# One encoder layer on one core: seven-product units in every down pair of two FFN parts, one cast and one store moved, two more dummy matmuls

## The chip, the cores and the metric

The kernel runs on one core of a Trainium2 chip. The metric is device time in microseconds (us). The kernel before took 1159.08 us in the median of three runs (1156.46 to 1161.56). One execution was profiled, and everything that is read from the trace below is of that one.

Engines are named as the profile names them: PE multiplies matrices (PEld is its load of weights, which overlaps the multiplication), DVE does element-wise vector work, ACT does casts, copies and activation functions, POOL is used here mainly to issue DMAs, and SP issues most of the DMAs.

## The reference, cut to what matters

One encoder layer over 256 tokens of width 2048, in float32. It has a mixing sub-layer (neighbourhood attention beside a recurrent block), then a dense SwiGLU feed-forward layer of inner width 5632, then a gated embedding. Only the feed-forward layer (FFN) is touched by the change, beside the first microseconds of the kernel:

```python
fn = rms_norm(h, g_ffn_pre[i])
ff = (jax.nn.silu(fn @ w_ffn_gate[i]) * (fn @ w_ffn_up[i])) @ w_ffn_down[i]
h = h + rms_norm(ff, g_ffn_post[i])
```

`w_ffn_gate` and `w_ffn_up` are 2048 x 5632, `w_ffn_down` is 5632 x 2048.

## The kernel before, in words

**Precision.** PE works here on a reduced 32-bit type. So each float32 operand is split into a rounded part and a remainder (`hi` and `lo` of the activations, `wh` and `wl` of the weights), and each block product takes three matmuls: hi x wh, lo x wh and hi x wl. One block product multiplies 128 tokens by 128 contraction rows by 512 columns. ACT makes `wh` with a cast (L630, `hi_stream`), DVE makes `wl` with a subtraction (L643, `lo_stream`), and both do it for each weight tile as it arrives. A weight tile is 128 partitions x 2 contraction blocks x 512 columns, 512 KB in float32.

**Groups.** The FFN is worked off in three parts of 4, 4 and 3 feature chunks of 512 (`PARTS`). In each part, every feature chunk f is one *group*: its gate chunk and its up chunk, accumulated together over 16 contraction blocks. Then follow two *down groups*, which multiply the part's features with `w_ffn_down`: the first makes output chunks 0 and 1 (c = 0), the second makes chunks 2 and 3 (c = 2). A group takes its contraction blocks two at a time. In a plain *pair*, two token tiles, two contraction blocks and two column chunks make eight block products (24 matmuls, `products`, L677 to L679). A *seven-product unit* makes the same result from seven block products (21 matmuls, `product`, L688 to L690) with sums and differences of blocks, in three pieces:

- `four_products`: four products, whose results are combined once per group by `made_of_four` (four DVE and two ACT operations on accumulators);
- `two_products`: two products;
- `one_product`: one product of each unit; the units 0 and 1 of a group share one weight tile here, unit 2 has its own.

The pieces of *four* are put among the last pairs of the group before (table `FOURS`: after how many pairs), the *two* and *one* pieces among the first pairs of their own group (table `TAKEN`). For its sums a unit needs three more DVE additions of 512 columns (L578, L582, L588, `sum_stream`), one DMA on POOL's queue that adds 256 KB of a weight block from memory to a block in the core (L599, `last_sum`), and seven blocks of weights to cast and subtract instead of four. It also needs sums of the activations: for the features of a part, `mid_sums` makes them with four DVE subtractions and a split (L1761, L306, L308).

Gate and up groups have three units from f = 2 on. Of the down groups, those of c = 0 have two units (contraction pairs 0 and 2 of the part) and those of c = 2 three (0, 2 and 4). In the last part c = 0 has two and c = 2 none.

**Features.** When a gate and up group ends, `up_post` makes the feature chunk on DVE, transposes it in 32 x 32 blocks (L334), and moves the blocks into place with sixteen small DMAs into the tile `mT` (L344, on POOL's queue). When the last has landed, `carried` casts `mT` into `mid0h` and `mid0l` (ACT L306, DVE L308; the digit is the part), and `mid_sums` follows. `mT` has one buffer: the next feature's DMAs wait until the sums of this one are made.

**Order.** Every engine works its queue in order. The order is written by a planner (`Plan`) while the program is built: each stream of work is a generator that yields its next operation with a modelled cost; `plan.add(..., ready)` says from when a task may be placed. For a DMA, `_run` sets the task's `ready` to the modelled start of that DMA, and `plan.now` is a scratch time that `done(event)` copies into an event and that is set anew when the task goes on. So the modelled times decide which cast stands ahead of which in ACT's queue; at run time an operation waits for its real data, and all that stand behind it on that engine wait too. There are five buffers for split weight tiles (`wh` and `wl` by fours, and `w`), so casts can run at most some tiles ahead of PE.

**Spill.** After the mixing sub-layer the residual `h` (two tiles of 1 MB) is stored to memory by `spill_h` (L1608), because its two buffers are used again: the first for loaded weight tiles called `lower` (the second tile of a four piece), the other for the sums of features (`sums`).

**Start.** `WARM` dummy matmuls on a constant tile run before the first weights are there (L2101). Each is executed in two passes.

Of the kernel before, what the change touches and what calls it, by code (L numbers as in the profile page):

```python
# [18 lines left out]
NT = S // P  # L19
# [18 lines left out]
PARTS = ((0, 4), (4, 8), (8, 11))  # L38
SEVEN_KS = (0, 2, 4)
RING = 5  # L40
DOWN_KS = {0: (0, 2), 2: (0, 2, 4)}
SEVEN_F = range(2, 11)

SWAPPED = [
    (lambda f: (("w_ffn_gate", f), ("w_ffn_up", f)), SEVEN_F, SEVEN_KS),
    *(
        (lambda c: (("w_ffn_down", c), ("w_ffn_down", c + 1)), (c,), [4 * f0 + k for k in ks])
        for f0, _ in PARTS for c, ks in DOWN_KS.items() if not c or f0 != PARTS[-1][0]
    ),
]  # L50

# [18 lines left out]
SOON = 2.0  # L70
ADDED = 6.0
AHEAD = 5
ISSUE = 160
WARM = 9


class Event:


    t = None  # L80
# [141 lines left out]
def dve(n, take=None, give=None):  # L222
    return ("dve", COST["dve"] + 0.00104 * n, None, take, give)
# [6 lines left out]
def dma(kb, take=None):  # L230
    return ("dma", kb / 340.0, None, take, None)
# [3 lines left out]
def layer(ctx: ExitStack, tc: tile.TileContext, a: dict, out: bass.AP):  # L235
# [3 lines left out]
    at = ctx.enter_context(tc.tile_pool(name="at", bufs=1))  # L239
    ps = ctx.enter_context(tc.tile_pool(name="ps", bufs=4, space=bass.MemoryType.PSUM))  # L240
    plan = Plan(wr=R_BUFS, w=W_BUFS, sm=SM_BUFS, acc=4, ev=1, mid=2, bt=2, m2=1, mt=1, sq=1, T0=1, T1=1, T4=1, **{f"{s}{j}": n for s, m, n in (("p", 5, 1), ("t", 3, 0)) for j in range(m)}, wr0=1, w0=1)
# [61 lines left out]
    def split(hi, lo, src, n, give=None):  # L303

        yield act(n)
        nc.scalar.copy(hi, src)  # L306
        yield dve(n, give=give)
        nc.vector.tensor_tensor(out=lo, in0=src, in1=f32(hi), op=ALU.subtract)  # L308
# [42 lines left out]
    def by_tile(v):  # L351
        return v.rearrange("p k (t q) -> p k t q", t=NT)
# [13 lines left out]
    def done(event):  # L366
        event.t = plan.now
# [47 lines left out]
    def seg(chunk, w, n0, lhs, ks, first=True, last=True, after=None):  # L415
        s = (chunk, lhs, ks, first, last, after, len(tiles))
        for k, _ in ks:
            tiles.append((w, k, n0))
        segs.append(s)
# [11 lines left out]
    class Group:  # L431
# [47 lines left out]
        def issue(self, nxt):  # L479
            if self.own is None:  # L480
                self.own = []
            self.twos = []
            if nxt:
                nxt.own = []
            n, m = len(self.rest), len(self.rest) - self.apart
            more = []
            for js in (range(0, 2), range(2, len(self.sevens))):
                more += [lambda j=j: self.two(j) for j in js if self.sevens]
            for js in (range(0, 2), range(2, len(self.sevens))):
                more += [lambda js=js: self.one(js)] if js and self.sevens else []  # L490
            taken = list(TAKEN.get((len(self.sevens), n), ()))

            def take():
                for _ in range(taken.pop(0) if taken else 0):
                    more.pop(0)()

            take()
            for i, k in enumerate(self.rest[:m]):
                for j, at in enumerate(FOURS[n, len(nxt.sevens)] if nxt and nxt.sevens else ()):
                    if i == at:  # L500
                        nxt.four(j)
                if i >= self.ahead:
                    self.pair(i)
                if nxt and nxt.apart and i == 1:
                    nxt.pair(0)
                    nxt.ahead = 1
                take()
            for ch, w, n0 in self.chunks if self.apart else ():
                seg(ch, w, n0, self.lhs, self.rest[m:], first=False)

    TAKEN = {(3, 5): (0, 2, 3), (2, 6): (0, 1, 1, 1), (2, 4): (0, 2, 1)}
    FOURS = {(8, 3): (3, 5, 7), (5, 3): (2, 3, 4), (6, 3): (3, 4, 5), (5, 2): (2, 4), (6, 2): (3, 5)}
    fours = {}

    raws, his, los = {}, {}, {}
# [290 lines left out]
    ev_unmerged = Event()  # L806
# [709 lines left out]
    def next_norm(sub, nxt, rstd, ev_rstd, g_next):  # L1516
# [51 lines left out]
        if sub is mix:  # L1568
            plan.add(spill_h(), plan.now)
# [28 lines left out]
        ).tile([NT, P, D], F32, name=f"part{i}")  # L1598
        for i in range(2)
    ]  # L1600
    ev_spilled, ev_back = Event(), Event()

    def spill_h():
        for e in hF.ev:
            yield e
        for t in range(NT):
            yield dma(1024)
            nc.sync.dma_start(spill[t], t2["h"].tiles[t])  # L1608
        done(ev_spilled)

    half_spill = ctx.enter_context(
        tc.tile_pool(name="half_spill", bufs=1, space=bass.MemoryType.DRAM)
# [51 lines left out]
    hF = Act()  # L1664
# [54 lines left out]
    def up_post(f, mid, kk0, g, soon):  # L1719

        def post(ch):
            yield g.free
            e = es.pop(f)
            for t in range(NT):
                yield dve(N)
                nc.vector.scalar_tensor_tensor(
                    out=e[:, t, :], in0=ch.accs[t], scalar=rstd_f[:, t : t + 1], in1=e[:, t, :],
                    op0=ALU.mult, op1=ALU.mult,
                )
            ch.release()  # L1730
            there = Event()
            mT = yield from moved(e, there, "mt", mT_tile, pool=(0, 2) if soon else range(4))
            plan.free["mid"].append(plan.now)
            yield there
            plan.add(carried(mid, kk0, mT), plan.now + (0.5 if soon else 3.0), -SOON if soon else 0.0)
        return post

    def carried(mid, kk0, mT):
        summed = any(kk0 <= kx < kk0 + 4 for kx in mid.ev_sums)
        for b in range(0, 4, 2):  # L1740
            kk = kk0 + b
            i, j = divmod(kk, 8)
            hi, lo = mid.tiles(i)
            yield from split(
                *(by_tile(x[:, j : j + 2, :]) for x in (hi, lo)), mT[:, b : b + 2], 2 * S,
                give="mt" if b and not summed else None,
            )
            mid.pair(kk)
        if summed:
            plan.add(mid_sums(mid, kk0, mT), plan.now + (20.0 if mid.name[-1] == str(2) else 0.0))  # L1750

    def mid_sums(mid, kk0, mT):

        yield ev_unmerged if kk0 else ev_spilled
        kxs = [kx for kx in DOWN_KS[2] if kk0 <= kx < kk0 + 4]
        m = 2 * len(kxs)
        a11, a12 = mT[:, 0:m:2, 0, :], mT[:, 1:m:2, 0, :]
        a21, a22 = mT[:, 0:m:2, 1, :], mT[:, 1:m:2, 1, :]
        for dst, x, y in ((a22, a21, a22), (a21, a21, a11), (a11, a11, a22), (a12, a12, a11)):
            yield dve(P * len(kxs))  # L1760
            nc.vector.tensor_tensor(out=dst, in0=x, in1=y, op=ALU.subtract)  # L1761
        if kk0 == 0:
            if "sums" not in t2:
                t2["sums"] = t2["pool"].tile([P, 2, 4, S], F32R, tag="h1", name="sums")
            hi, lo = (by_tile(t2["sums"][:, i, :, :]) for i in range(2))
        else:
            hi, lo = (
                by_tile(t2["s"][:, 2 + i, :].rearrange("p (k s) -> p k s", s=S)) for i in range(2)
            )
        yield from split(hi, lo, mT[:, 0:m], m * S, give="mt")  # L1770
        for i, kx in enumerate(kxs):
            mid.sums[kx] = {
                n: tuple(x[:, 2 * i + k, t, :] for x in (hi, lo))
                for n, k, t in (("S2", 0, 0), ("S7", 0, 1), ("S4", 1, 0), ("S1", 1, 1))
            }
            done(mid.ev_sums[kx])
# [76 lines left out]
    for part, (f0, f1) in enumerate(PARTS):  # L1853
        mid = Mid(f"mid{part}")
        last_part = part == len(PARTS) - 1
        for f in range(f0, f1):
            slot = ring()
            g = Chunk(gate_post(f), slot=slot)
            u = Chunk(up_post(f, mid, (f - f0) * 4, g, f == f1 - 1), late=(-3 if f == f1 - 1 else -1) * SOON, slot=slot)
            groups.append(Group(  # L1860
                [(g, "w_ffn_gate", f * N), (u, "w_ffn_up", f * N)], hF, KS,
                SEVEN_KS if f in SEVEN_F else (),
            ))
        ks = [(f0 * 4 + k, k) for k in range(0, (f1 - f0) * 4, 2)]
        for c in range(0, 4, 2):
            slot = ring()
            end = last_part and c
            groups.append(Group(
                [
                    (Chunk(  # L1870
                        sub_post(ffn, c + i, True, after_ffn) if last_part
                        else down_post(part, c + i), slot=slot,
                    ), "w_ffn_down", (c + i) * N)
                    for i in range(2)
                ],
                mid, ks, () if end else DOWN_KS[c], apart=2 if end else 0,
                after=load_sqrt if end else None,
            ))
    n_ffn = len(segs)
# [170 lines left out]
    n = 0  # L2050
# [47 lines left out]
    with tc.manual_schedule():  # L2098
        warm = bank("warm")
        for n in range(WARM):  # L2100
            nc.tensor.matmul(warm[:, 0, 0:P], ones, ones, start=True, stop=True)  # L2101
# [13 lines left out]
        chunk, lhs, ks, _, _, _, i0 = segs[-1]  # L2115
# [76 lines left out]
```

## Time and profile before

| what | us |
|---|---|
| median of three runs | 1159.08 |
| the profiled execution, whole | 1159.04 |
| span of its instructions | 1157.1 |
| PE busy in the span | 1144.7 |
| DVE busy | 903.7 |
| ACT busy | 711.1 |
| POOL busy | 133.5 |

The span counts from the first to the last instruction of the program; the time of the execution is 1.94 us longer. Times in the rows below are from the start of the span. In a timeline row the first number is the start and the second the time taken, both in us; `x2` means two such instructions merged; in square brackets stand the idle time of the engine before it and what ended that. The matmuls of one accumulation start at a distance of some 0.227 us, although each is listed with about 0.39 us, since they overlap. A row of the view by windows gives a stretch, its length, and for each engine the busy time and the number of instructions, then the granted PE clock (1.00 is full), the share of the DMA engines' time and GB/s.

### The profile page before, as it was taken

To read this page: it belongs to the slowest core of one execution; us is meant where nothing else is said; L and a number is where in the kernel's file an instruction comes from. 1 tells how busy PE (TensorE), PEld (TensorE's weight loads), DVE (VectorE), ACT (ScalarE), POOL (GpSimd) and SP (SyncE) were. 2 spreads that over 40 slices of the span, in tenths; PEclk is the share of its full clock that TensorE was granted. 3 is DMA by queue.
4 is the path that set the end of the run, shared out by engine and by line. 5 is a ranking of instruction groups with operands and counts; after the bars stand their busy time and mean duration, and the time that the engine had idled before them with its cause. 6 is when DMAs were issued, how large, how long until landed. Compare 5 with 4: busy or idle time off the path is not lost.

```text
span 1157.1 us, 15105 instructions
## 1 busy us (share of the span) xinstructions
PE 1144.7 (99%) x5213; PEld 949.7 (82%) x5213; DVE 903.7 (78%) x1133; ACT 711.1 (61%) x944; POOL 133.5 (12%) x214
## 2 busy tenths in 40 slices
PE   9999999999999989999999999999999999999997
PEld 8888888888888878888888888888888888787886
DVE  6678787888468758898877898978878887868575
ACT  7777777875557545565555556555455564655664
POOL 0000000000000032131110133212111303100000
PEclk9999999999999999999999999999999999999999
DMA  9867666545686977877876877776987787875671
GB/s 323 286 186 226 183 180 206 179 158 200 224 283 189 307 197 260 241 228 231 249 246 219 261 220 216 258 246 205 316 260 252 217 265 241 271 239 198 221 247 75
DMA packets 112285, 266.39 MB, mean 230 GB/s; under 512 B 39248, under 2 KB 46160, under 8 KB 110800
## 3 DMA queue, kind: packets, MB, share of 16 engines
q1 hardware_dynamic: 99568, 243.57, 61.9%
q0 software_dynamic: 12208, 21.51, 9.5%
q8 instruction: 41, 0.67, 0.2%
q10 hardware_dynamic: 432, 0.35, 0.1%
q14 instruction: 36, 0.29, 0.1%
HBM read 247.55 MB, written 9.44 MB: 222 GB/s over the span
## 4 chain that ended last, share of the span: by engine, by line
PE 93%; DMA 3%; DVE 1%; ACT 1%; POOL 1%; issue 1%; ACTq 0%; DVEq 0%
PE acc L678 24%; PE acc L679 24%; PE acc L677 24%; PE acc L690 5%; PE acc L689 5%; PE acc L688 5%; DMA mT<-mid 3%; PE tr L325 1%; POOL mT L344 1%; DMA wr<-in_w_ffn_gate 1%; DVE wl L643 0%; PE pg L356 0%; PE pg L357 0%; PE pg L355 0%; DVE h L1548 0%
## 5 line engine op out<-in xcount | busy, mean ns | idle before, releaser
L643 DVE TENSOR_TENSOR wl<-wr,wh 128x1024 fp32r<-128x1024 f32 (+1 forms) x309 | 369.7, 1210 | 117.0 <-ACT wh L630 113.5
L630 ACT CAST wh<-wr 128x1024 fp32r<-128x1024 f32 (+1 forms) x309 | 320.3, 1043 | 197.0 <-PE acc L678 142.7
L678 PE MATMUL acc<-wh,hT_mix_lo 128*128 128x512 f32 x400 | 155.8, 390 | 0.3 <-DVE hT_mix_lo L314 0.3
L677 PE MATMUL acc<-wh,hT_mix_hi 128*128 128x512 f32 x400 | 155.9, 390 | 0.0
L679 PE MATMUL acc<-wl,hT_mix_hi 128*128 128x512 f32 x400 | 155.6, 389 | 0.0
L344 POOL DMA_DIRECT2D mT<-mid x152 | 89.4, 599 | 555.3 <-DMA wr<-in_w_ffn_gate 400.9
L679 PE MATMUL acc<-wl,hT_hi 128*128 128x512 f32 x320 | 124.5, 390 | 0.0
L677 PE MATMUL acc<-wh,hT_hi 128*128 128x512 f32 x316 | 124.4, 394 | 0.0
L678 PE MATMUL acc<-wh,hT_lo 128*128 128x512 f32 x316 | 123.1, 390 | 0.0
L630 ACT CAST wh<-ple 128x1024 fp32r<-128x1024 f32 (+1 forms) x57 | 56.4, 992 | 76.4 <-DVE ple L582 42.9
L678 PEld LDWEIGHTS acc<-wh,hT_mix_lo 128*128 128x128 f32 x400 | 75.1, 188 | 16.5 <-DVE hT_mix_lo L314 1.0
L679 PEld LDWEIGHTS acc<-wl,hT_mix_hi 128*128 128x128 f32 x400 | 75.1, 188 | 15.6
L677 PEld LDWEIGHTS acc<-wh,hT_mix_hi 128*128 128x128 f32 x400 | 75.1, 188 | 15.5
L643 DVE TENSOR_TENSOR wl<-ple,wh 128x1024 fp32r<-128x1024 f32 (+1 forms) x57 | 65.3, 1147 | 13.0 <-ACT wh L630 12.5
L679 PEld LDWEIGHTS acc<-wl,hT_hi 128*128 128x128 f32 x320 | 60.1, 188 | 12.9
L678 PEld LDWEIGHTS acc<-wh,hT_lo 128*128 128x128 f32 x316 | 59.4, 188 | 11.5
L677 PEld LDWEIGHTS acc<-wh,hT_hi 128*128 128x128 f32 x316 | 59.4, 188 | 11.5
L599 POOL DMA_DIRECT2D ple<-in_w_ffn_up x27 | 24.0, 890 | 172.5 <-DVE wl L643 124.6
L643 DVE TENSOR_TENSOR wl<-third,wh 128x1024 fp32r<-128x1024 f32 x31 | 37.8, 1219 | 5.5 <-ACT wh L630 5.5
L630 ACT CAST wh<-third 128x1024 fp32r<-128x1024 f32 x31 | 32.6, 1051 | 14.8 <-PE acc L678 10.0
L678 PE MATMUL acc<-wh,hT_ffn_lo 128*128 128x512 f32 x104 | 40.8, 393 | 0.5 <-DVE hT_ffn_lo L314 0.5
L677 PE MATMUL acc<-wh,hT_ffn_hi 128*128 128x512 f32 x104 | 40.8, 392 | 0.0
(439 smaller groups left out, 2457.3 us busy)
## 6 DMA issues: line engine op xcount, KB each, us to landing
wr<-in_w_ffn_gate SPq DMA_DIRECT2D x78, 512.0 KB, 5.5
wr<-in_w_in SPq DMA_DIRECT2D x77, 512.0 KB, 4.4
wr<-in_w_ffn_down SPq DMA_DIRECT2D x62, 512.0 KB, 5.5
wr<-in_w_ffn_up SPq DMA_DIRECT2D x48, 512.0 KB, 5.2
wr<-in_w_out SPq DMA_DIRECT2D x32, 512.0 KB, 4.3
wr<-in_w_ple_gate SPq DMA_DIRECT2D x32, 512.0 KB, 4.5
lower<-in_w_ffn_up SPq DMA_DIRECT2D x22, 512.0 KB, 6.2
third<-in_w_ffn_down SPq DMA_DIRECT2D x14, 512.0 KB, 5.4
```

What stands on the lines that cost most here:

```text
L325: nc.tensor.transpose(tr[:, b, t * P : (t + 1) * P], e[:, t, sl], ident)
L344: (nc.gpsimd if i in pool else nc.sync).dma_start(dst[32 * j : 32 * j + 32, :, :, i, :], src[32 * i : 32 * i + 32, :, :, j, :],)
L599: nc.gpsimd.dma_start(dst, src, accum_op=ALU.add)
L630: nc.scalar.copy(his[i][:, 0 : src.shape[1], :] if n == 2 else his[i][:, j, :], src)
L643: nc.vector.tensor_tensor(out=los[i][:, m, :], in0=src, in1=f32(his[i][:, m, :]), op=ALU.subtract)
L677: nc.tensor.matmul(accs[t], hi[:, sl], his[i][:, j, :], start=st, stop=False, **group)
L678: nc.tensor.matmul(accs[t], lo[:, sl], his[i][:, j, :], start=False, stop=False, **group)
L679: nc.tensor.matmul(accs[t], hi[:, sl], los[i][:, j, :], start=False, stop=sp, **group)
L688: nc.tensor.matmul(dst, x[0], wh, start=start, stop=False, skip_group_check=seeded)
L689: nc.tensor.matmul(dst, x[1], wh, start=False, stop=False, skip_group_check=seeded)
L690: nc.tensor.matmul(dst, x[0], wl, start=False, stop=stop, skip_group_check=seeded)
```

## The change

- Down groups of the first two parts: c = 0 gets three units (0, 2 and 4), as c = 2 has. The last part stays as it was (two units in c = 0).
- The tables of places are keyed by the kind of group too. For a group whose left side is the features (a down group), three units are taken up as (0, 3, 2): all three *two* pieces after pair 0, both *one* pieces after pair 1; before, a down group with three units had (0, 2, 3), and one with two units and six pairs (0, 1, 1, 1). From down group to down group the *four* pieces stand ahead of pairs 3, 4 and 4; before, ahead of 3, 4 and 5 of six pairs. From the last gate and up group to a down group they stand ahead of 2, 3 and 4; before, 2 and 4.
- `carried` for feature chunk f = 0 alone is ready 12 modelled us after its move instead of 3.
- `spill_h` has an event for each of its two stores. Loads of `lower` wait for the first only, the sums of features for both; 40 is added to `plan.now` between the stores.
- `WARM` is 11 instead of 9.
- On the host, the blocks of `w_ffn_down` that the new units need are swapped (`SWAPPED`).

```diff
-DOWN_KS = {0: (0, 2), 2: (0, 2, 4)}
+DOWN_KS = (0, 2, 4)
 SEVEN_F = range(2, 11)
...
-        (lambda c: (("w_ffn_down", c), ("w_ffn_down", c + 1)), (c,), [4 * f0 + k for k in ks])
-        for f0, _ in PARTS for c, ks in DOWN_KS.items() if not c or f0 != PARTS[-1][0]
+        (
+            lambda c: (("w_ffn_down", c), ("w_ffn_down", c + 1)),
+            (0, 2) if f0 != PARTS[-1][0] else (0,),
+            [4 * f0 + k for k in (DOWN_KS if f0 != PARTS[-1][0] else DOWN_KS[:2])],
+        )
+        for f0, _ in PARTS
...
-WARM = 9
+WARM = 11
...
-            taken = list(TAKEN.get((len(self.sevens), n), ()))
+            taken = list(TAKEN.get((len(self.sevens), n, self.lhs is hF), ()))
...
-                for j, at in enumerate(FOURS[n, len(nxt.sevens)] if nxt and nxt.sevens else ()):
+                for j, at in enumerate(FOURS[n, len(nxt.sevens), (self.lhs is hF) + 2 * (nxt.lhs is hF)] if nxt and nxt.sevens else ()):
...
-    TAKEN = {(3, 5): (0, 2, 3), (2, 6): (0, 1, 1, 1), (2, 4): (0, 2, 1)}
-    FOURS = {(8, 3): (3, 5, 7), (5, 3): (2, 3, 4), (6, 3): (3, 4, 5), (5, 2): (2, 4), (6, 2): (3, 5)}
+    TAKEN = {(3, 5, True): (0, 2, 3), (3, 5, False): (0, 3, 2), (2, 4, False): (0, 2, 1)}
+    FOURS = {
+        (8, 3, 3): (3, 5, 7), (5, 3, 3): (2, 3, 4), (5, 3, 1): (2, 3, 4), (5, 3, 0): (3, 4, 4),
+        (5, 3, 2): (2, 3, 4), (5, 2, 1): (2, 4),
+    }
...
-    ev_spilled, ev_back = Event(), Event()
+    ev_spilled, ev_all_spilled, ev_back = Event(), Event(), Event()
...
-        for t in range(NT):
+        for t, ev in enumerate((ev_spilled, ev_all_spilled)):
             yield dma(1024)
             nc.sync.dma_start(spill[t], t2["h"].tiles[t])
-        done(ev_spilled)
+            done(ev)
+            plan.now += 40.0 if t == 0 else 0.0
...
-            plan.add(carried(mid, kk0, mT), plan.now + (0.5 if soon else 3.0), -SOON if soon else 0.0)
+            plan.add(carried(mid, kk0, mT), plan.now + (0.5 if soon else 3.0 if f else 12.0), -SOON if soon else 0.0)
...
-        yield ev_unmerged if kk0 else ev_spilled
-        kxs = [kx for kx in DOWN_KS[2] if kk0 <= kx < kk0 + 4]
+        yield ev_unmerged if kk0 else ev_all_spilled
+        kxs = [kx for kx in DOWN_KS if kk0 <= kx < kk0 + 4]
...
-                mid, ks, () if end else DOWN_KS[c], apart=2 if end else 0,
+                mid, ks, () if end else DOWN_KS[: 2 if last_part else 3], apart=2 if end else 0,
```

## The prediction

> **What bounds the kernel now.** I read the page's busy times and its chain of work first, then FFN stages by windows, then the timelines around every place where PE paused.
>
> ```profile
> span 1157.1 us, 15105 instructions
> PE 1144.7 (99%) x5213; PEld 949.7 (82%) x5213; DVE 903.7 (78%) x1133; ACT 711.1 (61%) x944; POOL 133.5 (12%) x214
> PE 93%; DMA 3%; DVE 1%; ACT 1%; POOL 1%; issue 1%; ACTq 0%; DVEq 0%
> ```
>
> PE bounds it: only 12.4 us of the span are without a matmul. So time goes in two ways: fewer matmuls, or a shorter pause. Three stages by windows give the price of a matmul: the down group c = 0 of part 0 (two units), the one of c = 2 (three units), and a gate and up group (three units).
>
> ```profile
> 511.46:553.62 42.16, 42.16 (x187) 34.91 (x186) 35.89 (x41) 24.17 (x28) 6.50 (x10) 1.00 0.77 240
> 553.62:595.10 41.48, 41.48 (x184) 34.35 (x183) 32.23 (x34) 24.44 (x27) 4.13 (x5) 1.00 0.77 245
> 678.06:719.54 41.48, 41.48 (x184) 34.35 (x183) 37.86 (x44) 25.46 (x29) 11.96 (x19) 1.00 0.77 237
> ```
>
> PE never rests in them. Six pairs and two units are 6 x 24 + 2 x 21 = 186 matmuls in 42.16 us; five and three are 183 in 41.48: 0.2267 us each. The only long pause of the FFN is at its first units. PE's timeline:
>
> ```profile
> 425.70 0.39 PE L679 MATMUL acc<-wl,hT_mix_hi 128*128 128x512 f32 x1
> 428.28 0.50 PE L688 MATMUL acc<-wh,sf 128*128 128x512 f32 x1 [2.19 <-ACT wh L630]
> 429.80 0.50 PE L690 MATMUL acc<-wl,sf 128*128 128x512 f32 x1 [0.79 <-DVE wl L643]
> 430.43 0.63 PE L689 MATMUL acc<-wh,sf 128*128 128x512 f32 x1
> 433.90 0.40 PE L677 MATMUL acc<-wh,hT_mix_hi 128*128 128x512 f32 x1
> ```
>
> Without a pause the next matmul would start at 425.70 + 0.23 = 425.93, and the twelve of this four piece would last 2.72 us. They end at 433.90: 7.97 - 2.72 = 5.25 us lost. About 3.3 are the two waits; the rest is slow running after them, 0.43 us a matmul instead of 0.23, with the granted clock down in this window:
>
> ```profile
> 430.00:435.00 5.00, 5.00 (x15) 3.58 (x15) 4.93 (x7) 4.23 (x5) 0.93 (x1) 0.66 0.58 119
> ```
>
> What PE waited for is in the timelines of ACT, DVE and POOL:
>
> ```profile
> 414.25 1.05 ACT L630 CAST wh<-third 128x1024 fp32r<-128x1024 f32 x1
> 424.40 1.14 ACT L306 CAST mid0h<-mT 128x512 fp32r<-128x512 f32 x2 [9.10 <-DMA mT<-mid]
> 427.18 1.04 ACT L630 CAST wh<-ple 128x1024 fp32r<-128x1024 f32 x1 [1.64 <-DVE ple L582]
> ```
> ```profile
> 425.05 0.69 DVE L308 TENSOR_TENSOR mid0l<-mT,mid0h 128x512 fp32r<-128x512 f32 x1 [8.12 <-ACT mid0h L306]
> 425.66 0.69 DVE L578 TENSOR_TENSOR ple<-wr 128x512 f32<-128x512 f32 x1
> 426.38 0.69 DVE L582 TENSOR_TENSOR ple<-ple,lower 128x512 f32<-128x512 f32 x1
> ```
> ```profile
> 402.68 4.73 POOL L344 DMA_DIRECT2D mT<-mid  x8 [400.91 <-DMA wr<-in_w_ffn_gate]
> 416.06 1.61 POOL L344 DMA_DIRECT2D mT<-mid  x2
> 455.58 8.85 POOL L344 DMA_DIRECT2D mT<-mid  x15 [12.27 <-DVE mid L334]
> ```
>
> The feature cast of f = 0 heads ACT's queue from 415.3, and its data lands at 424.4. For 9.1 us ACT does nothing; DVE stands 8.1 us behind its remainder, and the additions L578 and L582 and the cast L630 that PE needs stand behind both. The weights were not late. SP's queue and the page's table of issues:
>
> ```profile
> 381.36 0.42 SPq L1608 DMA_DIRECT2D h_spill<-h  x1
> 394.77 1.01 SPq L1608 DMA_DIRECT2D h_spill<-h  x1
> 409.62 0.44 SPq L538 DMA_DIRECT2D lower<-in_w_ffn_up  x1
> 416.96 0.33 SPq L538 DMA_DIRECT2D third<-in_w_ffn_up  x1
> 432.16 0.33 SPq L538 DMA_DIRECT2D wr<-in_w_ffn_gate  x1
> ```
> ```profile
> lower<-in_w_ffn_up SPq DMA_DIRECT2D x22, 512.0 KB, 6.2
> ```
>
> The `lower` of this unit was issued at 409.62; at 6.2 us it is there by 415.8, some ten before DVE used it. SP issued nothing from 416.96 to 432.16, as buffers were not freed.
>
> **The change part by part, against 1159.04 us of the profiled execution** (median 1159.08, so the same).
>
> *The cast of f = 0, nine modelled us later.* In ACT's queue it goes behind the casts that the stall held up. These need data of about 416 to 418: two additions of 0.69, a cast of 1.04 and its remainder are done by about 422, four before PE wants them at 425.93. The moved cast comes to ACT's head at about 415.3 + 9 = 424.3, when its data lands (424.4). Loads that now go on after 417 can delay the last moves (issued up to 417.7) by perhaps 3 us, which the tiles ahead cover. What is late next: `mid0l`, the sums, and with them the buffer `mT`. But in real time the cast hardly moves (424.4 before, some 425 after), so `mT` is free about as early as now; the next that takes it is the move of 455.58, thirty us on, and that is released by DVE's transpose. SP's and POOL's queues are passed by nothing. Ends: 0 if the wait only shifts, 5.25 if it goes. I take -5.25; the row it rests on shows data there and an engine held up by one instruction.
>
> *Two more units.* Each takes 24 - 21 = 3 matmuls from PE: 42.16 - 41.48 = 0.68 us, two of them -1.36, with nothing on PE to hide it. Each adds on DVE three additions of 0.69 and one and a half more tiles to subtract; the stage shows what that means: the c = 2 group, with three units, has DVE busy 32.23 of 41.48 us, and the gate and up group 37.86 of 41.48 with PE at 100%. The added load of `lower` replaces a plain tile's. The added POOL DMA (L599) has this row in the view of issues:
>
> ```profile
> ple<-in_w_ffn_down POOLq DMA_DIRECT2D x12, 256.0 KB, 4.6
> ```
>
> It has from the unit's remainder to the *one* piece: two pairs, three *two* pieces and a pair, 3 x 5.44 + 4.08 = 20.4 us, so 4.6 is hidden, also behind a store of a down chunk on POOL. The sums for the added units exist already, as c = 2 uses them.
>
> *Places (3, 4, 4) and (0, 3, 2).* No matmul is added, but a pair no longer parts the second and third four pieces, nor the *two* pieces. How far weights run ahead there shows in this tile of the third four piece of part 0's c = 2 (DVE and PE):
>
> ```profile
> 562.96 1.22 DVE L643 TENSOR_TENSOR wl<-ple,wh 128x1024 fp32r<-128x1024 f32 x1
> 569.94 0.39 PE L688 MATMUL acc<-wh,s 128*128 128x512 f32 x1
> ```
>
> Ready at 564.18, used at 569.94: 5.8 us ahead. Taking the pair away takes 5.44 us from PE and 2 x 1.22 from DVE, so the lead falls by 3.0 to 2.8. Three *two* pieces are 4.08 us of PE against 3 x 1.22 = 3.66 of DVE. I take 0; the upper end is the one stall that the trace shows, 5.25 at a place, and a gain is excluded, as PE does not pause there now.
>
> *The spill.* The 40 us do nothing, by the code: after a DMA the planner sets the task's `ready` to that DMA's modelled start, and the next operation is another DMA, no event that would read `plan.now`. So the stores should stay near 381 and 395. Only the first loads of `lower` are set free earlier, and the third unit's was issued after 432, long after both. I take 0. If the second store did go 40 us later, to about 435, the sums of features would wait for it until some 444 (an estimate: 6.2 us for 512 KB, half as much again for 1 MB), still ahead of 455.58; the lower end is 0 too, as the pause that 1 MB less would shorten is gone already.
>
> *Eleven dummies.* PE's first rows, and the cast that lets it start:
>
> ```profile
> 1.14 4.21 PE L2101 MATMUL warm<-ones 128*128 128x128 f32 x18 [1.14 <-POOL ones L290]
> 4.75 0.60 ACT L630 CAST wh<-wr 128x512 fp32r<-128x512 f32 x1
> 5.41 0.79 PE L669 MATMUL acc<-wh,hT_hi 128*128 128x512 f32 x1
> 6.85 0.48 PE L670 MATMUL acc<-wh,hT_lo 128*128 128x512 f32 x1
> 7.17 0.63 PE L679 MATMUL acc<-wl,hT_hi 128*128 128x512 f32 x2
> ```
>
> Eighteen passes take 4.21 us and end at 5.35, as the cast does. Four more are 4 x 0.234 = 0.94 us on PE's path. They stand where a matmul takes 0.43 us, until about 7.17, from where it takes 0.23: before, four real matmuls start in 5.41 to 7.17, after, two in 6.29 to 7.17, and two at full rate are 0.45 us. Ends: 0 (the first data lands later than here) and 0.94. I take +0.45. The Trainium skill speaks against this edit: "TensorE: Matmul & The Clock Gate", Part 1, says that warm-up is a span of time over free-running windows of some 3.4 us, not a number of matmuls, so dummies beyond the arrival of data buy nothing. By that rule the sum stays as it stands; the trace agrees so far that the rate rises while real work runs, after six us of unbroken PE work.
>
> *A second pause* is met by no edit, but lies behind all of them:
>
> ```profile
> 978.62 1.15 ACT L306 CAST mid2h<-mT 128x512 fp32r<-128x512 f32 x2 [5.78 <-DMA mT<-mid]
> 982.80 0.50 PE L688 MATMUL acc<-wh,sums 128*128 128x512 f32 x1
> 984.06 0.50 PE L690 MATMUL acc<-wl,sums 128*128 128x512 f32 x1 [0.53 <-DVE wl L643]
> 986.84 0.39 PE L677 MATMUL acc<-wh,hT_mix_hi 128*128 128x512 f32 x1
> ```
>
> Twelve matmuls in 4.04 instead of 2.72 us: 1.3 lost, the same way, at f = 9, whose cast keeps its 3 us. I take it as unchanged; the ends are -1.3 and +3.9 (grown to the first one's size).
>
> **Sum.** 1159.04 - 5.25 - 1.36 + 0.45 = 1152.9 us, 0.53% under the median.
>
> **The rivals.**
>
> *Half of it stays.* The cast still waits some 5 us, because the moves land later beside loads that no longer stop at 416.96. For it: a backlog of DMAs was what delayed them. Against it: PE then has four more tiles. Without the slow clock the loss is about 2.5: 1155.5.
>
> *A new wait takes the old one's place.* At one dense place, or grown at f = 9, ACT or DVE waits and PE pauses as at 425.93: 1152.9 + 5.25 = 1158.1, about no change. For it: the lead of 2.8 us is less than the 9.1 us that one cast could hold ACT. Against it: gate and up groups live with a fuller DVE.
>
> *Slower.* The same weights run dry at the dense places themselves: ahead of and inside both down groups of both parts, four places, each 5.25 with the clock. Two leave 1163.4, three give 1168.6; from three on it is slower by over 0.5%. For it: it is one pattern, so what fails once fails four times. Against it: DVE has 9 of 41 us free in the group that has three units already.
>
> *The spill does move.* Same time, 1152.9, as shown; it changes no chance.
>
> **How the numbers follow.** The sum as it stands 0.62, with a range of its own from 1150.8 (second pause gone, dummies hidden, and run noise) to 1154.8; half stays 0.09; a new wait 0.20; slower 0.09. The bound of 0.5% is 5.8 us, about what a measurement of this kernel can tell from no change, so faster means under 1153.3. The forecast lies only 0.4 below; of its 0.62 I give 0.53 to faster, and 0.02 to the fast tail of the case where half stays: 0.55. Same 0.36, slower 0.09. The range from 1150.5 to 1158.6 leaves out the slower case and the tails.
>
> **What would show it.** ACT's wait ahead of `mid0h` shrinks from 9.1 to under 2 us, with casts of weights ahead of it, PE runs through the first units at clock 1.00, and SP loads go on after 417. Both stages of the two c = 0 groups take 41.48 us with 183 matmuls. The stores stay near 381 and 395. The first real matmul starts about 6.3. I am wrong if PE shows idle time ahead of L688 or L690 in a down group, or if `mid0h` waits as long at another place.

## The result, and the profile after

The changed kernel took 1165.47 us in the median of six runs (1164.27 to 1166.77), the kernel before 1158.92 us beside it (six runs). The ratio is 1.005, with a 95% interval of 1.0035 to 1.0064: slower by about half a per cent, where 1152.9 us and a faster kernel had been forecast. The profiled execution took 1166.77 us, 7.73 more than that of before.

The page of the kernel after, its span, busy times and chain:

```profile
span 1164.7 us, 15123 instructions
PE 1143.6 (98%) x5211; PEld 948.3 (81%) x5211; DVE 909.8 (78%) x1143; ACT 714.1 (61%) x948; POOL 135.3 (12%) x216
...
PE 88%; DMA 4%; DVE 3%; ACT 2%; issue 1%; POOL 1%; SPq 0%; ACTq 0%; DVEq 0%
```

PE is busy 1.1 us less than before, and the span is 7.6 us longer. So what was to be saved in matmuls was saved, and a pause came from elsewhere. The two down groups of part 0 and of part 1, in windows from the first four piece of c = 0 to the first four piece of the next feature:

```profile
507.04:590.00 82.96, 82.96 (x367) 68.69 (x366) 68.70 (x74) 49.94 (x57) 11.52 (x16) 1.00 0.79 244
755.92:838.88 82.96, 82.96 (x367) 68.69 (x366) 71.44 (x79) 47.76 (x53) 12.92 (x18) 1.00 0.82 257
```

Before, the same stretch was 42.16 + 41.48 = 83.64 us, in part 0 as in part 1. It is 82.96 in both parts now: 0.68 us saved in each, with PE never at rest in the denser places. The pause near 426 us is gone too. ACT's timeline of the kernel after:

```profile
415.13 1.04 ACT L637 CAST wh<-third 128x1024 fp32r<-128x1024 f32 x1
419.24 1.05 ACT L637 CAST wh<-ple 128x1024 fp32r<-128x1024 f32 x1 [3.07 <-DVE ple L589]
...
426.82 1.05 ACT L637 CAST wh<-wr 128x1024 fp32r<-128x1024 f32 x1 [1.67 <-PE acc L685]
427.78 0.61 ACT L310 CAST mid0h<-mT 128x512 fp32r<-128x512 f32 x1
```

The cast of the first unit now stands ahead of `mid0h`, which waits for nothing when it comes to the head. PE starts that four piece without a wait: its first matmul starts at 426.80, 0.23 us after the one ahead of it.

The new pause is in the first down group of the last part, between the last matmul of a four piece (`sums`) and the next plain product (`mid2h`). PE's timeline of the kernel before at this place, then of the kernel after:

```profile
1000.21 0.39 PE L690 MATMUL acc<-wl,sums 128*128 128x512 f32 x1
1000.43 0.39 PE L677 MATMUL acc<-wh,mid2h 128*128 128x512 f32 x1
```

```profile
994.50 0.39 PE L697 MATMUL acc<-wl,sums 128*128 128x512 f32 x1
1004.18 0.79 PE L684 MATMUL acc<-wh,mid2h 128*128 128x512 f32 x1 [9.29 <-ACT wh L637]
...
1007.74 0.52 PE L685 MATMUL acc<-wh,mid2l 128*128 128x512 f32 x1
1008.09 0.40 PE L686 MATMUL acc<-wl,mid2h 128*128 128x512 f32 x1
```

From 994.50 to 1008.09 nine matmuls start, 2.04 us of work in 13.59: 11.55 us lost, 9.5 in the wait and the rest behind it, where a matmul takes 0.43 us instead of 0.23 and the granted clock is down (0.67 from 1004.2 to 1010). Followed back, in ACT's, SP's and DVE's timelines and in SP's own waits from 960 to 1000 us:

```profile
986.58 1.06 ACT L637 CAST wh<-lower 128x1024 fp32r<-128x1024 f32 x1
1003.08 1.04 ACT L637 CAST wh<-wr 128x1024 fp32r<-128x1024 f32 x1 [15.44 <-DMA wr<-in_w_ffn_down]
```
```profile
967.27 1.46 SPq L545 DMA_DIRECT2D wr<-in_w_ffn_down  x2
992.17 0.80 SPq L1834 DMA_DIRECT2D mg<-part  x2
993.02 0.43 SPq L545 DMA_DIRECT2D wr<-in_w_ffn_down  x1
```
```profile
990.92 1.22 DVE L650 TENSOR_TENSOR wl<-lower,wh 128x1024 fp32r<-128x1024 f32 x1
```
```profile
SPq L1834 <- DVE wl L650: 19.3, 1, 19.3
...
SPq L1834 <- DMA lower<-in_w_ffn_down: 4.0, 1, 4.0
```

ACT waits 15.4 us for a weight tile. Its load is issued at 993.02, and lands ten us later beside the others that were held back (in the kernel before, the loads issued from 985 to 1003 us took 4.9 us in the median). It stands in SP's queue behind `mg<-part`, the load of the partial down sums of the first two parts back into the core (`reload`). That load waits 23 us, until DVE has used the last unit's second tile: the remainder `wl<-lower` ends at 992.14, and `mg<-part` is issued at 992.17. In the kernel before, SP issued the same two loads with no wait ahead of its tile loads (the ten us behind them are a tile load that waits for its own buffer, 10.1 us for `wl`, which cost PE nothing):

```profile
974.19 0.33 SPq L538 DMA_DIRECT2D third<-in_w_ffn_down  x1
974.62 0.94 SPq L1826 DMA_DIRECT2D mg<-part  x2
985.77 6.48 SPq L538 DMA_DIRECT2D wr<-in_w_ffn_down  x4
```

The code gives the reason. The second tiles of the units lie in five places in turn, `lower[i] = (3, 4, 0, 1, 2)[n % RING]`, n counting the units from 0. Places 3 and 4 are in the buffer `mg0` (`lower_tile`), which `reload("mg", 0)` fills again. There were 39 units, and the last two, n = 37 and 38, took places 0 and 1. With 41, the last, n = 40, takes place 3. The planner does not know: `reload` takes no place of the ring, so its load keeps its spot right after the last gate and up group, while the buffer is busy until the last unit is split.

Against before, in the profiled executions: -5.25 (pause at 426) - 1.36 (two units) + 11.55 (new pause) + 1.75 (a wait in the next stage, told below) + 0.1 (f = 9) + 0.9 (later by this at the end of the mixing sub-layer, some 0.6 of it one wait at 210 us in the attention, whose code is not changed) = +7.7, as measured.

### The profile page after: what moved, and what is told of

It reads as the page before. It is cut to its first block, busy times and chain, and to the rows that moved or that the text cites. A ratio compares the mean times of both kernels' runs of the same rounds, so it can differ in the third digit from the quotient of the medians.

```text
span 1164.7 us, 15123 instructions
## 1 busy us (share of the span) xinstructions
PE 1143.6 (98%) x5211; PEld 948.3 (81%) x5211; DVE 909.8 (78%) x1143; ACT 714.1 (61%) x948; POOL 135.3 (12%) x216
## 4 chain that ended last, share of the span: by engine, by line
PE 88%; DMA 4%; DVE 3%; ACT 2%; issue 1%; POOL 1%; SPq 0%; ACTq 0%; DVEq 0%
PE acc L686 23%; PE acc L685 23%; PE acc L684 23%; PE acc L697 5%; PE acc L696 5%; PE acc L695 5%; DMA wr<-in_w_ple_gate 1%; DVE wl L650 1%; DMA mT<-mid 1%; ACT wh L637 1%; DMA wr<-in_w_ffn_down 1%; PE tr L329 1%; POOL mT L348 1%; DMA wr<-in_w_in 1%; DMA sq<-ev 0%
## 5 line engine op out<-in xcount | busy, mean ns | idle before, releaser
L685 PE MATMUL acc<-wh,hT_mix_lo 128*128 128x512 f32 x440 | 171.4, 390 | 0.3 <-DVE hT_mix_lo L318 0.3
L684 PE MATMUL acc<-wh,hT_mix_hi 128*128 128x512 f32 x440 | 171.4, 390 | 0.0
L686 PE MATMUL acc<-wl,hT_mix_hi 128*128 128x512 f32 x440 | 171.2, 389 | 0.0
L686 PE MATMUL acc<-wl,hT_hi 128*128 128x512 f32 x320 | 124.6, 390 | 0.0
L685 PEld LDWEIGHTS acc<-wh,hT_mix_lo 128*128 128x128 f32 x440 | 82.6, 188 | 18.0 <-DVE hT_mix_lo L318 1.0
L686 PEld LDWEIGHTS acc<-wl,hT_mix_hi 128*128 128x128 f32 x440 | 82.6, 188 | 17.1
L684 PEld LDWEIGHTS acc<-wh,hT_mix_hi 128*128 128x128 f32 x440 | 82.6, 188 | 17.1
L686 PEld LDWEIGHTS acc<-wl,hT_hi 128*128 128x128 f32 x320 | 60.0, 188 | 13.0 <-DVE wl L650 0.3
```

The costliest lines, as they stand in the source:

```text
L684: nc.tensor.matmul(accs[t], hi[:, sl], his[i][:, j, :], start=st, stop=False, **group)
L685: nc.tensor.matmul(accs[t], lo[:, sl], his[i][:, j, :], start=False, stop=False, **group)
L686: nc.tensor.matmul(accs[t], hi[:, sl], los[i][:, j, :], start=False, stop=sp, **group)
```

## The experiments

Theory A is the one above: a load that must wait heads SP's queue, because the added units turned the rotation. Theory B: weights run dry from the denser pieces, or the DMAs cannot feed them. Theory C: the moved cast or the spill's events cause it.

**E1, the changed kernel with the rotation turned by one.**

```diff
-        lower[i] = (3, 4, 0, 1, 2)[n % RING]
+        lower[i] = (2, 3, 4, 0, 1)[n % RING]
```

The last unit, n = 40, now takes place 2, which is in another buffer (`ple`).

> The changed kernel whole; only the order in which the units' second tiles rotate through their five buffers is turned by one, so that the last unit's tile (number 41) lies no longer in the memory that the partial down sums are loaded back into. Theory A (the load of the partial sums heads SP's queue and waits for the last unit's second tile, and the weight loads behind it wait too): the 9.7 us pause near 995 us is gone, the partial sums are loaded without a wait of over 5 us, and the time is 1153 to 1155 us. Theory B (weights run dry because units and pieces stand denser in the down groups, or the DMAs cannot feed them): the pause stays, 1163 to 1167 us. Theory C (the moved cast or the events of the spill cause it): the pause stays too, 1163 to 1167 us.

It took 1153.04 us (1152.32 to 1153.56), a ratio to before of 0.9942 (0.9929 to 0.9954). SP's timeline, and PE's at the place of the pause:

```profile
965.80 1.46 SPq L545 DMA_DIRECT2D wr<-in_w_ffn_down  x2
967.37 0.88 SPq L1834 DMA_DIRECT2D mg<-part  x2
978.36 0.33 SPq L545 DMA_DIRECT2D wr<-in_w_ffn_down  x1
```
```profile
992.80 0.39 PE L697 MATMUL acc<-wl,sums 128*128 128x512 f32 x1
993.03 0.39 PE L684 MATMUL acc<-wh,mid2h 128*128 128x512 f32 x1
```

The two loads of the sums go out at once, PE has no pause there, and the denser pieces, the moved cast and the spill's events are all still in it. B and C fall as causes of the new pause.

**E2, the kernel before with the rotation that puts its last tile there.**

```diff
-        lower[i] = (3, 4, 0, 1, 2)[n % RING]
+        lower[i] = (4, 0, 2, 3, 1)[n % RING]
```

The last unit, n = 38, now takes place 3.

> The kernel before, with nothing changed but the rotation: the last unit's second tile (number 39) now lies where the partial sums are loaded back. Theory A: a pause of 8 to 11 us and slow running after it appear in the first down group of the last part, 1168 to 1174 us. Theories B and C: no such pause, as nothing is denser and no cast or store is moved, 1157 to 1161 us.

It took 1171.24 us (1170.59 to 1172.09), a ratio of 1.0100 (1.0085 to 1.0115). SP's, DVE's and PE's timelines:

```profile
974.82 0.33 SPq L538 DMA_DIRECT2D third<-in_w_ffn_down  x1
998.42 0.81 SPq L1826 DMA_DIRECT2D mg<-part  x2
```
```profile
997.18 1.22 DVE L643 TENSOR_TENSOR wl<-lower,wh 128x1024 fp32r<-128x1024 f32 x1
```
```profile
1000.78 0.39 PE L690 MATMUL acc<-wl,sums 128*128 128x512 f32 x1
1010.12 0.80 PE L677 MATMUL acc<-wh,mid2h 128*128 128x512 f32 x1 [8.95 <-ACT wh L630]
```

With none of the change's own edits, the same pause appears at the same piece, and `mg<-part` goes out 0.02 us after the remainder ends (998.40).

**E3, the units and their places alone**, on the kernel before: `DOWN_KS`, `SWAPPED`, `TAKEN` and `FOURS` as in the change, nothing else.

> The kernel before with the two added units and the new places of the pieces alone (no moved cast, no new events of the spill, nine dummies). Theories A and B: the pause near 995 us is there and so is the one near 426 us (5.25 us): 1168 to 1173 us. Theory C: no pause near 995 us, 1157 to 1158 us.

It took 1170.81 us (1169.73 to 1172.74), a ratio of 1.0098 (1.0081 to 1.0114). PE's timeline has both pauses:

```profile
429.99 0.79 PE L695 MATMUL acc<-wh,sf 128*128 128x512 f32 x1 [2.83 <-ACT wh L637]
...
1010.67 0.79 PE L684 MATMUL acc<-wh,mid2h 128*128 128x512 f32 x1 [9.20 <-ACT wh L637]
```

So the units bring the new pause without the cast and the spill.

**E4, the cast alone**, on the kernel before:

```diff
-            plan.add(carried(mid, kk0, mT), plan.now + (0.5 if soon else 3.0), -SOON if soon else 0.0)
+            plan.add(carried(mid, kk0, mT), plan.now + (0.5 if soon else 3.0 if f else 12.0), -SOON if soon else 0.0)
```

> The kernel before with the cast of the first feature chunk nine modelled us later and nothing else. Theories A and B: the pause near 426 us goes, no pause near 995 us comes, 1153 to 1155 us. Theory C: the pause moves to near 995 us, 1160 us or more.

It took 1154.50 us (1154.31 to 1155.17), a ratio of 0.9957 (0.9943 to 0.9971): 5.2 us less than the 1159.72 of before beside it, by the interval between 3.4 and 6.6. In ACT's timeline the cast comes at

```profile
427.46 0.61 ACT L306 CAST mid0h<-mT 128x512 fp32r<-128x512 f32 x1
```

with no wait ahead of it.

**E5, the changed kernel with its own rotation, and the two loads later.**

```diff
         if i == last_two:
+            plan.add(reload("mg", 0), plan.clk["pe"] + 0.5)
+            plan.add(reload("mg", 1), plan.clk["pe"] + 1.5)
...
-        if i == mg1_end:
-            plan.add(reload("mg", 0), plan.clk["pe"] + 6.0)
-            plan.add(reload("mg", 1), plan.clk["pe"] + 14.0)
```

> The changed kernel with its own rotation; only the two loads of the partial sums are placed behind the last two_products piece, where the last unit's second tile is free already, instead of six and fourteen modelled us after the last gate and up group's pieces. Theory A (what costs the time is not where the tile lies but that a load which must wait heads SP's queue ahead of weight loads): the pause of 9.7 us near 995 us goes; 1153 to 1156 us, the upper end if the partial sums now come late for the first sums of the last part. If the two loads themselves, 2 MB among weight loads, are what the weights are late for: a pause of several us stays, 1158 us or more.

It took 1153.36 us (1151.60 to 1154.14), a ratio of 0.9942 (0.9928 to 0.9955). SP's timeline, with weight loads ahead of the first of the two:

```profile
981.49 5.31 SPq L545 DMA_DIRECT2D wr<-in_w_ffn_down  x3
...
994.95 0.43 SPq L1833 DMA_DIRECT2D mg<-part  x1
```

Here the last tile lies in `mg0` as in the changed kernel, and the partial sums come some 3 us later than there, without harm. So neither the place of the tile nor a late return of the sums costs anything by itself. What costs is that weight loads stand behind the one that waits.

**E6 and E7, eleven and nine dummies.** E6 is E1 once more; E7 is E1 with `WARM = 9`.

> The same kernel as e1_after_ring once more, so that the next two stand beside it on one chip: 1153.0 us, within 0.7.

> e1_after_ring with nine dummy matmuls instead of eleven. By the prediction's term (0.45 us for two more dummies, between 0 and 0.94): 1152.6 us, 0.1 to 0.9 us under e6_after_ring_again. If the free-running clock decides and the extra dummies run where PE would wait: no difference, 1153.0.

E6 took 1153.18 us (1152.00 to 1154.00), a ratio of 0.9939 (0.9927 to 0.9952); E7 1154.77 us (1152.55 to 1156.40), 0.9951 (0.9939 to 0.9964). The intervals overlap, so the times show neither a gain of the dummies nor the forecast cost. PE's first rows of E6, then of E7:

```profile
1.14 4.97 PE L2109 MATMUL warm<-ones 128*128 128x128 f32 x22 [1.14 <-POOL ones L294]
5.85 0.48 PE L676 MATMUL acc<-wh,hT_hi 128*128 128x512 f32 x1
...
8.70 0.39 PE L684 MATMUL acc<-wh,hT_hi 128*128 128x512 f32 x1
```
```profile
1.14 4.21 PE L2109 MATMUL warm<-ones 128*128 128x128 f32 x18 [1.14 <-POOL ones L294]
6.05 0.79 PE L676 MATMUL acc<-wh,hT_hi 128*128 128x512 f32 x1 [0.71 <-ACT wh L637]
...
10.06 0.40 PE L677 MATMUL acc<-wh,hT_lo 128*128 128x512 f32 x1
...
10.76 0.39 PE L684 MATMUL acc<-wh,hT_hi 128*128 128x512 f32 x1
```

**E8, E1 with the cast of f = 9 nine modelled us later too.**

```diff
-3.0 if f else 12.0
+3.0 if f % 9 else 12.0
```

> e1_after_ring, with the cast of the features of f = 9 nine modelled us later too, as the change does for f = 0. If the pause at the first units of the last part's down group (1.3 us lost in the kernel before) is the same thing as the one near 426 us: ACT's wait for the moved features shrinks from 6 us to under 2, PE no longer pauses there, 1151.7 to 1152.3 us. If the cast only waits elsewhere: 1153 or more.

It took 1151.82 us (1151.17 to 1152.14), a ratio to before of 0.9928 (0.9916 to 0.9940). That is the lowest median of all here, clearly under the kernel before and the changed one. It is 1.4 us under E6 beside it, but the ranges of these two touch (E6 from 1152.00, E8 up to 1152.14). ACT's timeline has no wait ahead of the cast any more:

```profile
977.61 1.06 ACT L637 CAST wh<-wr 128x1024 fp32r<-128x1024 f32 x1 [0.26 <-PE acc L696]
978.57 0.61 ACT L310 CAST mid2h<-mT 128x512 fp32r<-128x512 f32 x1
```

PE goes from the plain products (L686, 976.05) to the first unit (L695, 976.27) without a wait. So the pause at the last part's units was the same thing as the one at 426 us.

## Why the prediction was wrong, by its steps

- **The cast of f = 0: right in mechanism and size.** -5.25 was taken; E4 gives -5.2 (3.4 to 6.6). The cast came at 427.8 in the changed kernel instead of 424.3, and the tiles ahead covered that.
- **Two more units: the product term right, the step wrong.** The stages are 0.68 us shorter each, as forecast. The step that failed is the sentence "The added load of `lower` replaces a plain tile's", and with it that the units add nothing but what stands in their own groups. A unit also takes a turn of a rotation over five buffers. Two more of them moved every later unit by two places, as far as the last part, whose own code is untouched, and there the last one met a buffer with another use due. It is a term that the sum lacked, of +11.55 us, more than all the gains. The sign of being wrong that the prediction named, idle time of PE ahead of L688 or L690, would not have shown it either: PE stopped ahead of a plain product, for a plain tile. The count of units and the list of places were both in the code before.
- **The places of the pieces: right.** No pause in either down group, in both parts.
- **The spill: right.** The stores went out at 382.37 and 394.58 (381.36 and 394.77 before). With that edit alone on the kernel before, the program that is built has the same instructions in the same order on every engine.
- **Eleven dummies: the size not borne out, the sign open.** A cost of 0.45 was taken from one profile in which dummies and data ended together. In the changed kernel the first real matmul came at 5.41 as before, not at about 6.3, for the clock rose sooner there (4.5 us instead of 7.0): its 22 passes took 4.30 us, not 5.1. In E5 and E8, where it rose at 6.6 and 7.2, the dummies did hold the first real matmul until 5.85, although its cast was done at 5.33 and 5.31: so the mechanism of the term is there, with a start 0.44 us later where it had 0.94. Where data is late, as in E7, the extra dummies stand where PE would rest. The times of E6 and E7 do not decide between the two.
- **The second pause: right**, unchanged in the changed kernel (1.4 us). It is 0.8 to 1.5 us long in every profile but that of E8, where it is gone.
- **The rivals.** "A new wait takes the old one's place" came nearest in kind, but put the wait at casts in the dense groups or at f = 9, and its price was 5.25. The slower rival named the wrong mechanism (weights run dry in the dense groups); its bound of three pauses was too high, as one pause of twice the length did it. E1, the change without the rotation's accident, took 1153.04 us where 1152.9 was forecast. Its two main terms are there; that it comes so near is luck: in its profile the FFN began 0.6 us sooner than before, where the dummies' term had 0.45 later, and the stage after the FFN lost 0.9 that the sum did not have, which about cancel.

What stays open: a wait of PE in the stage after the FFN, for moved blocks of the residual, cost 2.1 us in the changed kernel and 0.34 before. PE's timeline of the kernel after:

```profile
1100.30 0.49 PE L684 MATMUL acc<-wh,hT_ffn_hi 128*128 128x512 f32 x1 [1.52 <-ACT hT_ffn_hi L316]
```

It is between 0.3 and 1.3 us in the profiles of E1 to E8 and does not follow the edits there; its cause is not known.

## What to carry to other kernels

When a change adds steps to a rotation of buffers, number them to the last one and ask which buffer each later step now gets, and what else is due there: the price can fall in a stage that the diff does not touch. A DMA that has to wait for its destination is better not queued ahead of loads that need not wait, on the same queue; look at the waits of the queue itself, for the engines' waits named only the load that came late. Where an engine works in order, an operation that waits for data of uncertain arrival belongs behind those whose data is there.

## What the runs showed that was not expected

The first rise of PE's clock, seen where the distance of the matmuls halves, is not tied to the count of dummies: in the ten profiles it came between 4.5 and 10.1 us after the start, with PE at work from 1.14 us on in all of them. The 25th real matmul started between 11.44 and 13.49 us in the five with nine dummies, and between 11.05 and 11.98 in the five with eleven. The two ranges overlap, and of the late ones with nine, E3's (12.79) also had a wait of 0.96 us for a weight; so only E7 speaks for more dummies.

The Trainium skill says in "TensorE: Matmul & The Clock Gate", Part 1, that the window which decides is free-running, so that the point of the rise varies from run to run, by half a microsecond to either side. These profiles agree that it varies, but show more: 3.4 to 6.0 us after PE's first pass in nine of them, and 8.9 in E7. In the prediction another sentence of the Trainium skill there, that warm-up is a span of time and no number of matmuls, was read as a case against the dummies, of which that Part says nothing. E7 shows what that reading left out: a rest of 0.71 us between the dummies and late data, and half the rate until about 10 us. Whether that rest delayed the rise, one profile can't tell.
